# A two-layer attention trunk: gate sums and their biases issued earlier, `mem` loaded with `x`, GpSimd's distances held back

## The chip, the cores and the metric

The kernel runs on one core of one Trainium2 chip. The metric is the device time of one execution in microseconds (us), the median of three runs. The engines are TensorE (PE, matrix products), VectorE (DVE), ScalarE (ACT), GpSimd (POOL) and SyncE (SP, which here only issues transfers). Each engine runs its own instructions in order and waits on semaphores for the others.

## What is computed

A decoder trunk of two layers over 256 tokens of width 1024, all in float32:

```python
for i in range(DEPTH):                      # 0: forgetting attention (FoX), 1: block attention with ALiBi
    xn = rms_norm(h, norm_mix[i]); mn = rms_norm(mem, norm_mem[i])
    mk, mv = halves of mn @ w_mem_kv[i]     # 4 memory heads
    q, k, v, f_logit, qm = parts of xn @ w_in
    # FoX: log_f = log_sigmoid(f_logit + b_fgate); F = cumsum(log_f)
    #      logit[t, s] = q_t.k_s / 8 + F[t] - F[s], causal, softmax, times v      (12 heads)
    # MoBA with one block of 256: logit[t, s] = q_t.k_s / 8 - slope * (t - s), causal
    # memory: softmax(qm.mk / 8) @ mv
    h = h + concat(heads) @ w_out[i]
    gu = rms_norm(h, norm_ffn[i]) @ w_gate_up[i]
    h = h + (silu(gate) * up) @ w_down[i]
return rms_norm(h, norm_final)
```

## The kernel before

**Weights.** All weights lie in one stream in the order of their use, cut into units of 1 MB (128 partitions by 2048). `fetch` issues one unit from SP's queue into one of four buffers with the tag `raw`; the trace names them raw0, raw1 and so on. Products are made from split operands: `split` makes of each half unit a high part `hi` (a copy on ACT, L215) and a rest `lo` (a subtraction on DVE, L216). `weights` hands out a row of a unit and keeps five half units split ahead; `prod` turns each product into three: high by high, low by high, high by low. Units 5 and 6 are the first q and k group, 7 is `memT` (the transposed memory tokens, split into `x_mem`, L237 and L238), 8 and 9 the memory key and value weights, 10 is `mem` itself (only for its row norms), 11 the memory queries, 12 to 15 the second and third q and k groups.

**Order.** PE and SP run their instructions as the program writes them (`manual_schedule`). For DVE, ACT and POOL a scheduler at build time chose the order. Attention heads are generators (`attend`), kept in the list `active`; `step()` lets each of them go to its next `yield`, and is called after every second row of a q and k product. So score products, transposes and value products lie between the rows of the big products, and `IDLE` and `IDLE_MEM` say how many steps a pair of heads sits out.

**The first layer's mixer.** First the v products (they carry the 12 gate columns too), with the squared sums of `x` (`factor`: a Square on ACT with its sum, `me` on DVE, a power on POOL). From the gate columns come z, na, e, l and lf (log f). Then the first q and k group, `memory_heads` (the memory key and value products, the memory queries), and two more q and k groups. `gate_sums` is appended after the first q and k group: two products F (cumulative sums by row), a copy `fr`, a write of `fr` to DRAM (`fd`), three broadcast reads of it into `fk` (128 partitions by 12 heads by 256), and the products Fq with the copy `fq`. The write and the reads are on SP's queue, the reads behind the landing of the write. `bias` of a pair of heads then takes four DVE instructions (L510): fk minus fq plus mask, of 128 columns for the first query half into a buffer `bias`, of 256 for the second in place. In the second layer `bias` is two POOL instructions on `fk` (L505, distance times slope), which the scheduler has put in the first layer's attention, as soon as a pair's `fk` is free.

**Memory heads.** `mk` (L349) is the product of the memory keys and the spread factor `rsb_mem`; eight ACT copies and four subtractions (two on DVE, two on POOL) split it, four copies and four subtractions split the queries `xqm`, and the score product `s_m` of the first memory pair needs them. It stands in PE's program after the fourth row of the second q and k group.

```python
ENG = (nc.gpsimd, nc.vector)
def step():
    for g in list(active):
        if next(g, "end") == "end":
            active.remove(g)
```

Of the kernel before, what the change touches and what calls it, by code (L numbers as in the profile page):

```python
# [64 lines left out]
def _constants():  # L65


    i = np.arange(P)
    ident = np.eye(P, dtype=np.float32)
    prefix = np.concatenate(  # L70
        [np.where(i[:, None] <= i[None, :], -1.0, 0.0), np.full((P, P), -1.0)], axis=1
    ).astype(np.float32)
    dist = i[:, None] + P - np.arange(2 * P)[None, :]
    mask = np.where(dist < 0, NEG, 0.0).astype(np.float32)
    dist = np.where(dist < 0, 3e38, dist).astype(np.float32)
    return np.concatenate([ident, prefix, mask, dist], axis=1)


class Plan:


    def __init__(self, a):
# [5 lines left out]
        for i in range(2):  # L88
# [5 lines left out]
            for g in range(3):  # L94
                if g == MEM_AT[i]:
                    if i == 0:
                        U["memT", 0] = self.unit([memT], 0, KD, 0, S)
                        self.mkv(a, 0)
                        self.blocks.append(a["mem"][0].reshape(NT, P, D).transpose(1, 0, 2).reshape(-1))
                        self.shapes.append((NT, 1, D))  # L100
                        U["mem"] = len(self.shapes) - 1
# [37 lines left out]
def trunk(ctx: ExitStack, tc: tile.TileContext, plan, stream, x, gains, norm_final, b_fgate, square, out):  # L139
# [14 lines left out]
    prefix = sq[:, P:3 * P]  # L154
    mask = sq[:, 3 * P:5 * P]
    dist = sq[:, 5 * P:7 * P]
# [26 lines left out]
    raw_only = {U["xT"], U["memT", 0], U["memT", 1], U["mem"]}  # L183
# [66 lines left out]

    def inverse_root(ms, more, name):
# [4 lines left out]
        nc.gpsimd.tensor_tensor(rs, me, minus_half, op=ALU.pow)  # L256
# [49 lines left out]
    fk = cp.tile([P, H, S], F32, name="fk")  # L306
    mks = [cp.tile([P, 2, 2 * S], F32R, name=f"mk{p}") for p in range(HM // 2)]
# [15 lines left out]
    def mem_kv(i):  # L323
# [117 lines left out]
    def mixer(i, xs, rs):  # L441
# [14 lines left out]
        for k, t in order:  # L456
            v_tile(k, t)
            if i == 0 and (k, t) == (FACTORS_AT, 1):
                rs.extend(factor(h[t_], f"x0{t_}") for t_ in range(NT))
        if i == 0:  # L460
# [22 lines left out]
        def gate_sums():  # L483
            yield
            fb = bank("F_ps")
            fb.mm(fb.t[:H, 0:S], lf[:, 0], prefix)
            fb.mm(fb.t[:H, P:S], lf[:, 1], prefix[:, 0:P], stop=True)
            fr = ap.tile([P, 2, S], F32, tag="work", name="fr", bufs=WORK_BUFS)[:H, 0]
            nc.vector.tensor_copy(fr, fb.t[:H, :S])
            nc.sync.dma_start(fd, fr)  # L490
            for g in range(GATE_PARTS):
                hs = slice(g * (H // GATE_PARTS), (g + 1) * (H // GATE_PARTS))
                nc.sync.dma_start(fk[:, hs], fd[hs].unsqueeze(0).to_broadcast([P, H // GATE_PARTS, S]))
            gb = bank("Fq_ps")
# [291 lines left out]
```

## Time and profile before

| | |
|---|---|
| device time, median of 3 runs | 628.02 us (627.84 to 628.21) |
| profiled execution, its own time | 628.5 us |
| its span | 626.7 us |
| PE busy | 610.7 us, 97% of the span |
| DVE busy | 456.9 us, 73% |
| ACT busy | 393.1 us, 63% |
| POOL busy | 60.5 us, 10% |

The span is the profiled stretch from the first to the last instruction; the 1.8 us to its own time lie around it. PE is busy nearly throughout, so the idle time that is left on PE, and where, is what the rows below look at. The first layer's mixer runs from the start to about 130 us, its feed-forward layer to about 316 us, then follows the second layer.

### The profile page before, as it was taken

To read this page: it belongs to the slowest core of one execution; us is meant where nothing else is said; L and a number is where in the kernel's file an instruction comes from. 1 tells how busy PE (TensorE), PEld (TensorE's weight loads), DVE (VectorE), ACT (ScalarE), POOL (GpSimd) and SP (SyncE) were. 2 spreads that over 40 slices of the span, in tenths; PEclk is the share of its full clock that TensorE was granted. 3 is DMA by queue.
4 is the path that set the end of the run, shared out by engine and by line. 5 is a ranking of instruction groups with operands and counts; after the bars stand their busy time and mean duration, and the time that the engine had idled before them with its cause. 6 is when DMAs were issued, how large, how long until landed. Compare 5 with 4: busy or idle time off the path is not lost.

```text
span 626.7 us, 9569 instructions
## 1 busy us (share of the span) xinstructions
PE 610.7 (97%) x3636; PEld 532.8 (85%) x3636; DVE 456.9 (73%) x827; ACT 393.1 (63%) x734; POOL 60.5 (10%) x90
## 2 busy tenths in 40 slices
PE   7999899999999999999999999999999999999995
PEld 6999887788888888888899999877888888888884
DVE  5588999977667676668675689986866666666664
ACT  6789888575555555557467499865755555555542
POOL 2022354300000000000011032200000000000000
PEclk9999999999999999999999999999999999999998
DMA  8985731445555545555445642332455555555301
GB/s 291 369 313 196 311 135 69 157 140 216 170 191 201 195 171 177 197 202 187 166 186 202 246 146 80 135 134 101 158 182 198 202 188 173 185 193 202 136 0 67
DMA packets 17638, 112.31 MB, mean 179 GB/s; under 512 B 2220, under 2 KB 2744, under 8 KB 5432
## 3 DMA queue, kind: packets, MB, share of 16 engines
q1 hardware_dynamic: 17304, 111.42, 49.3%
q8 instruction: 28, 0.46, 0.3%
q10 hardware_dynamic: 288, 0.29, 0.1%
q14 instruction: 18, 0.15, 0.1%
HBM read 110.64 MB, written 1.06 MB: 178 GB/s over the span
## 4 chain that ended last, share of the span: by engine, by line
PE 83%; DVE 7%; ACT 5%; issue 2%; DMA 2%; POOL 0%; SPq 0%; POOLq 0%; ACTq 0%; DVEq 0%
PE gu L178 39%; PE d_acc L178 18%; PE qk_ps L178 8%; PE v_ps L178 5%; PE o_acc L178 5%; DMA raw<-in_stream 2%; DVE lo L216 2%; PE s_s L178 1%; ACT hi L215 1%; PE mv_ps L178 1%; PE qm_ps L178 1%; PE mk_ps L178 1%; ACT p_s L406 1%; ACT xq L362 1%; PE s_m L178 1%
## 5 line engine op out<-in xcount | busy, mean ns | idle before, releaser
L216 DVE TENSOR_TENSOR lo<-raw,hi 128x1024 fp32r<-128x1024 f32 (+3 forms) x201 | 240.6, 1205 | 74.0 <-ACT hi L215 68.9
L215 ACT ACTIVATE hi<-raw 128x1024 fp32r<-128x1024 f32 (+3 forms) x201 | 206.4, 1035 | 76.8 <-PE d_acc L178 47.8
L178 PE MATMUL gu<-x_ffn,hi 128*128 128x512 f32 x704 | 250.0, 398 | 0.4 <-DVE x_ffn L238 0.3
L178 PE MATMUL gu<-x_ffn,lo 128*128 128x256 f32 x704 | 198.3, 282 | 0.0
L178 PEld LDWEIGHTS gu<-x_ffn,hi 128*128 128x128 f32 x704 | 132.2, 188 | 33.3 <-DVE x_ffn L238 1.4
L178 PEld LDWEIGHTS gu<-x_ffn,lo 128*128 128x128 f32 x704 | 132.9, 189 | 1.0 <-ACT x_ffn L237 0.3
L178 PE MATMUL d_acc<-hi,h 128*128 128x512 f32 x348 | 107.7, 390 | 0.0
L178 PEld LDWEIGHTS d_acc<-hi,h 128*128 128x128 f32 x348 | 65.4, 188 | 13.7
L178 PE MATMUL qk_ps<-x_x,hi 128*128 128x256 f32 x384 | 72.3, 284 | 0.0
L178 PE MATMUL d_acc<-lo,h 128*128 128x512 f32 x174 | 68.0, 391 | 0.0
L178 PEld LDWEIGHTS qk_ps<-x_x,hi 128*128 128x128 f32 x384 | 60.9, 192 | 0.8 <-issue 0.8
L178 PE MATMUL qk_ps<-x_x,lo 128*128 128x256 f32 x192 | 54.4, 283 | 0.0
L641 ACT ACTIVATE gate<-gu 128x256 f32<-128x256 f32 x44 | 16.9, 384 | 58.9 <-PE gu L178 58.9
L641 ACT ACTIVATE up<-gu 128x256 f32<-128x256 f32 x44 | 16.9, 385 | 41.1 <-PE gu L178 40.9
L178 PE MATMUL o_acc<-hi,x_hT 128*128 128x512 f32 x128 | 41.8, 405 | 0.6 <-DVE x_hT L235 0.3
L178 PEld LDWEIGHTS d_acc<-lo,h 128*128 128x128 f32 x174 | 32.7, 188 | 7.0
L642 DVE TENSOR_TENSOR gate<-gu,gate 128x256 f32<-128x256 f32 x44 | 18.7, 424 | 27.1 <-ACT gate L641 27.1
L642 DVE TENSOR_TENSOR up<-gu,up 128x256 f32<-128x256 f32 x44 | 18.7, 425 | 26.1 <-ACT up L641 26.1
L178 PEld LDWEIGHTS qk_ps<-x_x,lo 128*128 128x128 f32 x192 | 36.8, 192 | 0.0
L178 PE MATMUL v_ps<-hi,x_x 128*128 128x384 f32 (+1 forms) x128 | 33.6, 344 | 0.6 <-ACT hi L215 0.6
L178 PEld LDWEIGHTS o_acc<-hi,x_hT 128*128 128x128 f32 x128 | 22.8, 188 | 6.4 <-issue 1.3
L406 ACT ACTIVATE p_s<-p_s,nmax_s 128x128 f32<-128x128 f32 (+1 forms) x48 | 21.4, 447 | 10.5 <-DVE nmax_s L396 10.3
(152 smaller groups left out, 751.5 us busy)
## 6 DMA issues: line engine op xcount, KB each, us to landing
raw<-in_stream SPq DMA_DIRECT2D x95, 1024.0 KB, 4.8
raw<-in_stream SPq DMA_DIRECT2D x4, 768.0 KB, 4.9
raw<-in_stream SPq DMA_DIRECT2D x2, 780.0 KB, 8.8
fk<-fd SPq DMA_DIRECT2D x3, 512.0 KB, 5.1
raw<-in_stream SPq DMA_DIRECT2D x3, 390.0 KB, 5.8
h<-in_x SPq DMA_DIRECT2D x2, 512.0 KB, 9.2
raw<-in_stream SPq DMA_DIRECT2D x1, 512.0 KB, 7.4
gfin<-in_norm_final SPq DMA_DIRECT2D x1, 512.0 KB, 3.4
```

Of the source, the lines that this page charges most:

```text
L178: nc.tensor.matmul(o, lhsT, rhs, start=self.fresh, stop=stop, skip_group_check=True)
L215: nc.scalar.activation(hi[:, c0:c1], src[:, c0:c1], AF.Copy)
L216: nc.vector.tensor_sub(lo[:, c0:c1], src[:, c0:c1], hi[:, c0:c1].bitcast(F32))
L362: nc.scalar.activation(dst[HOME[a], a], q[HOME[a]], AF.Copy)
L406: nc.scalar.activation(pr[:, a, c], src, AF.Exp, bias=nmax[:, a, j], scale=scale, accum_out=total[:, a, j])
L641: nc.scalar.activation(v[:, 1], b[s].t[:, S:], AF.Copy)
L642: nc.vector.tensor_add(v[:, 0], b[s].t[:, :S], v[:, 1])
```

## The change

It has four parts. The generator `gate_sums` is appended before the first q and k group, sits out two steps, and issues F, Fq and the write `fd` after the sixth of its eight rows; one step later it issues the three reads into `fk`; then each of six steps issues the four bias instructions of one pair, into a buffer of its own for the first half (`first_bias`). The write and the reads move from SP's queue to POOL's. The second half of the constant `prefix` (all -1) becomes a broadcast of one column. `mem` leaves the stream of units: it is loaded behind `x` into two buffers with the tag `probs`, its squared sums come right after those of `x`, and its factor is spread right after that of `x`. POOL's distances for the second layer may be issued only after the sixth power on POOL (`powers[5]`, the second factor of the first feed-forward layer). The tag of one small buffer changes (`"f"` to `"x"`).

```diff
     def load_x():
         for t in range(NT):
             nc.sync.dma_start(h[t], x[0, t * P:(t + 1) * P, :])
+        for t in range(NT):
+            nc.sync.dma_start(mem_t[t], mem[0, t * P:(t + 1) * P, :])
         nc.sync.dma_start(sq, square)
...
-        nc.gpsimd.tensor_tensor(rs, me, minus_half, op=ALU.pow)
+        powers.append(nc.gpsimd.tensor_tensor(rs, me, minus_half, op=ALU.pow))
...
-        if i == 0:
-            fetch_to(U["mem"] + 1)
-            rs_mem.extend(factor(raws[U["mem"]][:, t, 0], f"mem{t}") for t in range(NT))
-            rsb_mem.append(spread(rs_mem, "mem", (1.0,), "mem")[:, 0, :])
...
                 rs.extend(factor(h[t_], f"x0{t_}") for t_ in range(NT))
+                rs_mem.extend(factor(mem_t[t_], f"mem{t_}") for t_ in range(NT))
...
         def gate_sums():
+
+            yield
             yield
             fb = bank("F_ps")
-            fb.mm(fb.t[:H, 0:S], lf[:, 0], prefix)
-            fb.mm(fb.t[:H, P:S], lf[:, 1], prefix[:, 0:P], stop=True)
+            fb.mm(fb.t[:H, 0:P], lf[:, 0], prefix, stop=True)
+            fb.mm(fb.t[:H, P:S], lf[:, 0], minus_one.to_broadcast([P, P]))
+            fb.mm(fb.t[:H, P:S], lf[:, 1], prefix, stop=True)
             fr = ap.tile([P, 2, S], F32, tag="work", name="fr", bufs=WORK_BUFS)[:H, 0]
             nc.vector.tensor_copy(fr, fb.t[:H, :S])
-            nc.sync.dma_start(fd, fr)
-            for g in range(GATE_PARTS):
-                hs = slice(g * (H // GATE_PARTS), (g + 1) * (H // GATE_PARTS))
-                nc.sync.dma_start(fk[:, hs], fd[hs].unsqueeze(0).to_broadcast([P, H // GATE_PARTS, S]))
+            nc.gpsimd.dma_start(fd, fr)
...
             nc.scalar.activation(fq.rearrange("p t h -> p (t h)"), gb.t[:, :NT * H], AF.Copy)
+            yield
+            for g in range(GATE_PARTS):
+                hs = slice(g * (H // GATE_PARTS), (g + 1) * (H // GATE_PARTS))
+                nc.gpsimd.dma_start(fk[:, hs], fd[hs].unsqueeze(0).to_broadcast([P, H // GATE_PARTS, S]))
+            for h0 in range(0, H, 2):
+                yield
+                for j in range(h0, h0 + 2):
+                    for t, o in ((0, first_bias), (1, fk)):
+                        nc.vector.scalar_tensor_tensor(o[:, j], fk[:, j, :(t + 1) * P], fq[:, t, j:j + 1], mask[:, P - t * P:],
+                                                       op0=ALU.subtract, op1=ALU.add)
...
             b = fk[:, h0:h0 + 2]
-            if i == 1:
+            if i == 0:
+                return first_bias[:, h0:h0 + 2], b
+
+            with tc.issue_after(powers[NT * 3 - 1].ins):
                 for a in range(2):
                     nc.gpsimd.tensor_scalar(b[:, a], dist, -float(slopes[h0 + a]), NEG, op0=ALU.mult, op1=ALU.max)
-                return b[:, :, P:], b
...
             kb = [bank(f"qk_ps{i}{2 * g + a}") for a in range(2)]
+            if i == g == 0:
+                active.append(gate_sums())
...
                 rsb = spread(rs, f"x{i}", (DH ** -0.5, 1.0), "x")
                 if i == 0:
-                    active.append(gate_sums())
+                    rsb_mem.append(spread(rs_mem, "mem", (1.0,), "mem")[:, 0, :])
```

The orders that the scheduler chose change with it. On ACT, at the end of the v products (`v0`, `v1` are the scaled v, `e`, `l`, `na` the gate's small tiles, `hi6` the split of the second half of the first q and k group), before:

```order
L477 ACTIVATE v0_80<-v_ps000_144,rs_x00_295 128x384
L477 ACTIVATE v1_81<-v_ps010_146,rs_x01_302 128x384
L467 ACTIVATE e_329<-na_327 128x24
L469 ACT_TABLE_LOAD
L469 ACTIVATE l_331<-e_329 128x24
L215 ACTIVATE hi6_0_258<-raw6_166 128x1024
L215 ACTIVATE hi6_2_274<-raw6_166 128x1024
L237 ACTIVATE x_mem0_499<-raw7_188,gT_72 128x256 x8
```

and ACT at the same place in the change:

```order
L476 ACTIVATE v0_84<-v_ps000_151,rs_x00_302 128x384
L476 ACTIVATE v1_85<-v_ps010_153,rs_x01_309 128x384
L244 ACTIVATE junk_mem0_311,ms_mem0_312<-mem0_82 128x1024
L244 ACTIVATE junk_mem1_318,ms_mem1_319<-mem1_83 128x1024
L467 ACTIVATE na_348<-na_348 128x24
L468 ACT_TABLE_LOAD
L468 ACTIVATE na_348<-na_348 128x24
L216 ACTIVATE hi6_0_265<-raw6_173 128x1024
L216 ACTIVATE hi6_2_281<-raw6_173 128x1024
L238 ACTIVATE x_mem0_536<-raw7_195,gT_72 128x256 x7
L497 ACTIVATE fq_358<-Fq_ps_455 128x24
L238 ACTIVATE x_mem0_536<-raw7_195,gT_72 128x256
```

The two squared sums of `mem` now stand ahead of the gate's exponential and of the split `hi6`, and the copy `fq` stands inside the splits of the memory tokens. On DVE the two `me_mem` likewise stand ahead of the two `z`.

On DVE ahead of `mk0` (the product of memory keys and factor, which the first memory scores need), before:

```order
L216 TENSOR_TENSOR lo12_0_543<-raw12_371,hi12_0_542 128x1024
L216 TENSOR_TENSOR lo12_2_589<-raw12_371,hi12_2_588 128x1024
L254 TENSOR_SCALAR me_mem1_717<-ms_mem1_715 128x1
L216 TENSOR_TENSOR lo13_0_621<-raw13_429,hi13_0_620 128x1024
L216 TENSOR_TENSOR lo13_2_650<-raw13_429,hi13_2_649 128x1024
L216 TENSOR_TENSOR lo14_0_680<-raw14_431,hi14_0_679 128x1024
L216 TENSOR_TENSOR lo14_2_757<-raw14_431,hi14_2_756 128x1024
L349 TENSOR_TENSOR mk0_726<-mk_ps0_506,rsb_mem_724 128x512
```

and DVE there in the change:

```order
L217 TENSOR_TENSOR lo11_2_620<-raw11_327,hi11_2_619 128x1024
L506 SCALAR_TENSOR_TENSOR fk_87<-fk_87,fq_358,sq_74 128x256
L506 SCALAR_TENSOR_TENSOR first_bias_88<-fk_87,fq_358,sq_74 128x128 x2
L506 SCALAR_TENSOR_TENSOR fk_87<-fk_87,fq_358,sq_74 128x256 x2
L217 TENSOR_TENSOR lo12_0_656<-raw12_390,hi12_0_655 128x1024
L506 SCALAR_TENSOR_TENSOR first_bias_88<-fk_87,fq_358,sq_74 128x128 x2
L506 SCALAR_TENSOR_TENSOR fk_87<-fk_87,fq_358,sq_74 128x256 x2
L217 TENSOR_TENSOR lo12_2_689<-raw12_390,hi12_2_688 128x1024
L506 SCALAR_TENSOR_TENSOR first_bias_88<-fk_87,fq_358,sq_74 128x128 x2
L506 SCALAR_TENSOR_TENSOR fk_87<-fk_87,fq_358,sq_74 128x256 x2
L217 TENSOR_TENSOR lo13_0_723<-raw13_460,hi13_0_722 128x1024
L349 TENSOR_TENSOR mk0_750<-mk_ps0_543,rsb_mem_502 128x512
```

Between `lo8_0` (the first split of the memory weights) and `mk0` there now stand 20 of the 24 bias instructions, ten of each width, and eleven `lo`, two `qk`, four subtractions of q and k; before, no bias stood there, and twelve `lo`. (Units are numbered one lower from 11 on, since `mem` left the stream.)

On POOL, behind the last power of `mem`, in the change (`xq00`, `xk00` are subtractions for the first pair's q and k):

```order
L259 TENSOR_TENSOR rs_mem1_323<-me_mem1_321,minus_half_78 128x1
L492 DMA fd_86<-fr_452 12x256
L501 DMA fk_87<-fd_86 128x1024
L501 DMA fk_87<-fd_86 128x1024 x2
L364 TENSOR_TENSOR xq00_506<-qk00_504,xq00_506 64x256
L372 TENSOR_TENSOR xk00_507<-qk00_504,xk00_507 64x256
```

Before, POOL went from the powers of `x` straight to these subtractions; now the write and the three reads stand ahead of them, and the first read waits for the write. The twelve distances stand behind the powers of the first feed-forward layer.

## Rows read from the trace of the kernel before

**Rows 1.** Page, part 1: busy us, share of the span, instructions.

```profile
PE 610.7 (97%) x3636; PEld 532.8 (85%) x3636; DVE 456.9 (73%) x827; ACT 393.1 (63%) x734; POOL 60.5 (10%) x90
```

**Rows 2.** PE's waits from 25 to 130 us: total us, times, longest.

```profile
PE s_m L178 <- POOL xqm L364: 2.0, 1, 2.0
PE s_s L178 <- DVE pT_s L421: 0.8, 1, 0.8
PE o_m L178 <- ACT pT_m L420: 0.4, 1, 0.4
PE s_s L178 <- DVE nmax_s L396: 0.3, 1, 0.3
PE o_acc L178 <- DVE nmax_s L396: 0.2, 1, 0.2
```

**Rows 3.** Busy time by window: PE, PEld, DVE, ACT, POOL, PEclk, DMA share, GB/s.

```profile
26.00:28.00 2.00, 2.00 (x19) 2.00 (x18) 1.24 (x4) 1.58 (x3) 0.00 (x0) 1.00 0.99 418
...
80.00:100.00 20.00, 19.34 (x145) 16.07 (x144) 19.55 (x58) 15.59 (x43) 10.05 (x11) 1.00 0.30 107
```

**Rows 4.** Timeline of ACT: start, us, instruction, idle before it.

```profile
25.07 1.27 ACT L477 ACTIVATE v<-v_ps,rs_x 128x384 f32<-128x384 f32 x2 [0.17 <-POOL rs_x L256]
26.74 0.22 ACT L467 ACTIVATE e<-na 128x24 f32<-128x24 f32 x1 [0.41 <-DVE na L465]
...
28.41 1.99 ACT L215 ACTIVATE hi<-raw 128x1024 fp32r<-128x1024 f32 x2
30.55 3.31 ACT L237 ACTIVATE x_mem<-raw,gT 128x256 fp32r<-128x256 f32 x8 [0.15 <-DMA raw<-in_stream]
...
48.25 1.05 ACT L243 ACTIVATE junk_mem<-raw 128x1024 bf16<-128x1024 f32 x1
```

**Rows 5.** Timeline of PE.

```profile
30.76 0.38 PE L178 MATMUL qk_ps<-x_x,lo 128*128 128x256 f32 x1
...
42.77 0.82 PE L178 MATMUL F_ps<-sq,lf 128*12 128x256 f32 x4
43.52 0.84 PE L178 MATMUL Fq_ps<-lf,sq 128*128 128x12 f32 x6
...
64.22 1.18 PE L178 MATMUL s_m<-mk,xqm 128*128 128x256 f32 x8 [2.05 <-POOL xqm L364]
```

**Rows 6.** Timeline of DVE.

```profile
25.73 0.37 DVE L463 SCALAR_TENSOR_TENSOR z<-v_ps,rs_x,bfg 128x12 f32<-128x12 f32 x2 [0.64 <-POOL rs_x L256]
...
53.67 4.63 DVE L216 TENSOR_TENSOR lo<-raw,hi 128x1024 fp32r<-128x1024 f32 x4 [0.87 <-ACT hi L215]
58.22 0.69 DVE L349 TENSOR_TENSOR mk<-mk_ps,rsb_mem 128x512 f32<-128x512 f32 x1
...
107.63 0.61 DVE L510 SCALAR_TENSOR_TENSOR bias<-fk,fq,sq 128x128 f32<-128x128 f32 x2
108.16 0.87 DVE L510 SCALAR_TENSOR_TENSOR fk<-fk,fq,sq 128x256 f32<-128x256 f32 x2
```

**Rows 7.** Timeline of SP's queue, and landing of the reads into fk.

```profile
52.73 0.43 SPq L490 DMA_DIRECT2D fd<-fr  x1
58.54 1.30 SPq L493 DMA_DIRECT2D fk<-fd  x3
...
DMA to landing us min/median/max: 4.2/5.1/6.2
```

**Rows 8.** Timeline of DVE and of POOL where the two run at once or alone.

```profile
41.16 0.84 DVE L364 TENSOR_TENSOR xq<-qk,xq 64x256 fp32r<-64x256 f32 x1
62.45 0.42 DVE L372 TENSOR_TENSOR mk<-mk,mk 64x256 fp32r<-64x256 f32 x1 [0.81 <-ACT mk L369]
93.29 1.22 DVE L216 TENSOR_TENSOR lo<-raw,hi 128x1024 fp32r<-128x1024 f32 x1
...
40.12 1.60 POOL L364 TENSOR_TENSOR xq<-qk,xq 64x256 fp32r<-64x256 f32 x1 [14.40 <-ACT xq L362]
92.97 2.47 POOL L505 TENSOR_SCALAR fk<-sq 128x256 f32<-128x256 f32 x2 [2.17 <-issue]
```

More of the change, by code (lines that the diff above doesn't have):

```diff
@@ L69, in _constants @@
     ident = np.eye(P, dtype=np.float32)
-    prefix = np.concatenate(
-        [np.where(i[:, None] <= i[None, :], -1.0, 0.0), np.full((P, P), -1.0)], axis=1
-    ).astype(np.float32)
+    prefix = np.where(i[:, None] <= i[None, :], -1.0, 0.0).astype(np.float32)
     dist = i[:, None] + P - np.arange(2 * P)[None, :]
@@ L138, in trunk @@
 @with_exitstack
-def trunk(ctx: ExitStack, tc: tile.TileContext, plan, stream, x, gains, norm_final, b_fgate, square, out):
+def trunk(ctx: ExitStack, tc: tile.TileContext, plan, stream, x, mem, gains, norm_final, b_fgate, square, out):
     nc = tc.nc
@@ L153, in trunk @@
     ident = sq[:, 0:P]
-    prefix = sq[:, P:3 * P]
-    mask = sq[:, 3 * P:5 * P]
-    dist = sq[:, 5 * P:7 * P]
+    prefix = sq[:, P:2 * P]
+    mask = sq[:, 2 * P:4 * P]
+    dist = sq[:, 4 * P:6 * P]
     slopes = _slopes()
@@ L160, in trunk @@
     nc.gpsimd.memset(minus_half, -0.5)
+    minus_one = cp.tile([P, 1], F32, name="minus_one")
+    nc.gpsimd.memset(minus_one, -1.0)
+    mem_t = [ap.tile([P, 2, 512], F32, tag="probs", name=f"mem{t}", bufs=3).rearrange("p a s -> p (a s)") for t in range(NT)]
     def load_x():
@@ L182, in trunk @@
     U = plan.U
-    raw_only = {U["xT"], U["memT", 0], U["memT", 1], U["mem"]}
+    raw_only = {U["xT"], U["memT", 0], U["memT", 1]}
     halves = [(i, j * (sh[0] // 2), sh[0] // 2) for i, sh in enumerate(plan.shapes) if i not in raw_only for j in range(2)]
@@ L306, in trunk @@
     fk = cp.tile([P, H, S], F32, name="fk")
+    first_bias = cp.tile([P, H, P], F32, name="first_bias")
     mks = [cp.tile([P, 2, 2 * S], F32R, name=f"mk{p}") for p in range(HM // 2)]
@@ L496, in gate_sums @@
                 for u in range(t + 1):
-                    gb.mm(gb.t[:, t * H:(t + 1) * H], prefix[:, (t - u) * P:(t - u + 1) * P], lf[:, u], stop=u == t)
+                    gb.mm(gb.t[:, t * H:(t + 1) * H], prefix if u == t else minus_one.to_broadcast([P, P]), lf[:, u], stop=u == t)
             nc.scalar.activation(fq.rearrange("p t h -> p (t h)"), gb.t[:, :NT * H], AF.Copy)
+            yield
[8 more added lines that the diff above has]
+                                                       op0=ALU.subtract, op1=ALU.add)
         def bias(h0):
             b = fk[:, h0:h0 + 2]
-            if i == 1:
+            if i == 0:
+                return first_bias[:, h0:h0 + 2], b
+            with tc.issue_after(powers[NT * 3 - 1].ins):
                 for a in range(2):
                     nc.gpsimd.tensor_scalar(b[:, a], dist, -float(slopes[h0 + a]), NEG, op0=ALU.mult, op1=ALU.max)
-                return b[:, :, P:], b
-            b0 = ap.tile([P, 2, P], F32, tag="bias", name=f"bias{h0}", bufs=1)
-            for a in range(2):
-                for t, o in ((0, b0), (1, b)):
-                    nc.vector.scalar_tensor_tensor(o[:, a], b[:, a, :(t + 1) * P], fq[:, t, h0 + a:h0 + a + 1], mask[:, P - t * P:],
-                                                   op0=ALU.subtract, op1=ALU.add)
-            return b0, b
+            return b[:, :, P:], b
         hT = xposed(f"hT{i}")
@@ L634, in gu @@
             if first:
-                rsb.append(spread(rs, f"f{i}", (1.0,), "f")[:, 0])
+                rsb.append(spread(rs, f"f{i}", (1.0,), "x")[:, 0])
             if kk == 0:
@@ L774 @@
     arrays = {
-        "stream": np.concatenate(plan.blocks), "x": a["x"], "gains": gains,
+        "stream": np.concatenate(plan.blocks), "x": a["x"], "mem": a["mem"], "gains": gains,
         "norm_final": a["norm_final"], "b_fgate": a["b_fgate"], "square": square,
```

12 lines of the change are left out of this document (4 added, 8 removed).

## The prediction

> **What bounds the kernel now.** I read the page first: PE is busy for 610.7 of 626.7 us [rows 1], so nothing but PE's idle time can be won. The list of PE's waits between 25 and 130 us says where it is in the first mixer: 2.05 us before the first memory scores `s_m`, and later 0.8, 0.4, 0.3 and 0.2 us, behind DVE or ACT [rows 2]. The windows show why the later ones are there: from 80 to 100 us DVE is busy for 19.55 of 20 us, so the attention heads go at DVE's pace [rows 3]. All that an earlier gate chain can win here is 2.05 + 1.7 = 3.75 us.
>
> The second thing to see is how tight the queues are ahead of that. In the first q and k group PE uses the low half of unit 6 at 30.76 [rows 5]. ACT began that unit's split at 28.41 [rows 4], and a split half takes about 1.0 us on ACT (1.99 for two) and 1.14 on DVE (four in the 4.55 us from 53.67 to 58.22) [rows 4, 6]. So PE takes it the moment it is there, and whatever delays ACT here delays PE.
>
> **What the change costs, step by step.**
>
> *Squares of `mem` ahead of the gate.* ACT ends its two v copies at 26.34 [rows 4]. Now two squares of 1.05 follow, to 28.44. DVE's two `me_mem` stand ahead of `z`, so `z` waits for them, and with it, queued behind on DVE, the scaled v and `na`, for which ACT's exponential waits. From `z` (25.73) to the exponential (26.74) took 1.01 us, from there to the split of unit 6 1.67 us [rows 4, 6]. So the split starts at 28.44 + 0.05 + 1.01 + 1.67 = 31.2 instead of 28.41, and PE gets the low half at 33.5: **2.7 us of new idle time**, in a place where there was none. Could the load of `mem` make it worse? It is 1 MB in front of units 6 and 7, less 64 KB of the smaller constants: 0.98 MB at 418 GB/s [rows 3] is 2.4 us. Unit 7 landed at 30.55, since ACT waited for it [rows 4]; unit 6, a megabyte ahead, at about 28.0. With 2.4 us more it lands at 30.4, before ACT comes to it: hidden, by 0.8 us. Squares and factor no longer stand among the memory products; there ACT and DVE win about 2 us, but see what is late next.
>
> *F and Fq* cost PE 1.45 us (42.77 to 43.52, and from there as long again less 0.1) [rows 5] and only change place. The product with the broadcast column has as many columns as the half of `prefix` that it replaces: nothing, plus at most 0.1 us for one more instruction. The new spread of `mem`'s factor is the old one, earlier.
>
> *ACT and DVE up to the memory weights.* ACT ends unit 6 at 33.2, seven splits of `x_mem` (3.31 us for eight [rows 4]) at 36.1, and then `fq` makes it wait for PE: 23 products of 0.12 us after 33.5, F and Fq, 37.7. The last `x_mem` and the first half of unit 8 bring it to 39.1, and DVE starts `lo8_0` at 39.2.
>
> *The biases ahead of `mk`.* This is the dear part. From `lo8_0` to `mk` DVE now has eleven splits of 1.14 (12.5 us), ten biases of 128 columns at 0.265 (107.63 to 108.16 for two) and ten of 256 at 0.40 (0.87 for two, less the overlap of the next) [rows 6], 6.6 us, two `qk` of 0.6, 1.2 us, and four subtractions of 0.42 [rows 8], 1.7 us. Two of the four ran at 0.84 when POOL subtracted beside them [rows 8]; POOL's own four come a little later now and meet splits and biases instead, so I leave the 0.85 us in. Sum 22.9 us of work; my count of the moments when ACT has not yet delivered gives 1.6 us of waiting. So `mk` starts at 39.2 + 22.9 + 1.6 = 63.7, against 58.22 [rows 6].
>
> *From `mk` to `s_m`.* Behind `mk` DVE still has `qm` 0.6, two splits 2.3, two subtractions 0.85, four biases 1.3 and the subtraction for `xqm` 0.4, with `mk` itself 6.1 us; with 0.3 of waiting 6.4 us, against 6.0 before (58.22 to 64.22 [rows 5, 6]). ACT's copies for it run beside. So `s_m` starts at 70.1. The same sum made for the kernel before gives 64.6 where the trace has 64.22, so I take 0.4 off: **69.7, that is 5.5 us later.** PE itself would be there at 64.9 (64.22 less its wait of 2.05, and the 2.7 lost above), so its wait grows from 2.05 to about 4.8 us. Queued behind the waiting `s_m` in PE's program is everything else of the layer.
>
> *After that* DVE has less to do than before, by some 7 us of biases and plus two splits that were put off, so the waits of 0.8, 0.4, 0.3 and 0.2 us should go: **1.7 us back**, or nothing if the put-off splits fill the room.
>
> *POOL and SP.* The reads into `fk` wait on POOL for the write, and behind them stand POOL's first subtractions, needed only by the first self scores after `s_m`: free. `fr` is there at 37.5. Before, 5.8 us went by from the issue of the write to that of the reads, and the reads took 4.2 to 6.2 us to land [rows 7]. What POOL takes to issue a transfer no row shows; the bounds are these rows and 3 us more (the 1.30 us of SP's three issues, doubled). By the rows the first part of `fk` lands at 47.5, the last at 49.5 to 50.8; DVE comes to the first bias at 48.7, so I take no wait. Units 10 to 14 come earlier, since SP no longer waits on `fd` and no buffer is held by `mem`; the work that needs them is late anyway.
>
> *The distances* leave the mixer, where POOL is no bottleneck, and put 12 × 1.2 us [rows 8] on POOL beside the feed-forward layer, where PE sets the pace. A DVE split that ran under two distances took 1.22 us, no longer than others [rows 8]. I take zero; with every distance blocking DVE it would be 14 us of DVE time, spread over a layer in which the splits are five half units ahead.
>
> On this the Trainium skill has a rule (SBUF — State Buffer, "SBUF: two separate sides"): DVE and GpSimd share a port pair as an exclusive lock, taken by a DVE instruction with two SBUF inputs against a GpSimd instruction that reads SBUF, and the later one waits for the whole other. The split beside two distances disagrees, the subtraction of 0.84 beside POOL's 1.60 fits [rows 8].
>
> **The sum.** +5.5 − 1.7 = +3.8 us. The profiled execution took 628.5 us and would take 632.3; it lies 0.5 above the median of 628.02, so the forecast is **631.8 us**, 0.6% slower.
>
> **Rivals.**
>
> 1. *The mixer gets its cover (not slower).* If `mk` starts by 58.5, `s_m` is ready when PE is (64.9), both kinds of wait go, and only the 2.7 us remain: 628.0 − 3.75 + 2.7 = 626.9. For it speaks that ACT no longer waits for a load and for `rsb_mem` ahead of `mk`. Against it: DVE enters at 39.2 and has 22.9 us of work before `mk`, 3.6 us too much without any waiting. It needs the scheduler's bias instructions to run much shorter than their rows. The break-even is `mk` at 60.0. If the delay of 2.7 did not show either, it would be 624.3.
> 2. *The delay at unit 6 is overlapped.* If `z` did not sit behind `me_mem`, or ACT made up for it, everything starts 2 to 2.7 us earlier: 629.1 to 629.8, or no difference with the later waits gone as well.
> 3. *`fk` lands late.* With POOL's issues at 3 us more, the first bias waits 1 to 4 us, DVE holds `mk` back by the same, and the time is 633 to 636.
> 4. *POOL's subtractions block DVE.* Four that each hold DVE for 0.8 us (half of the 1.60 that one took beside DVE [rows 8]) in place of the 0.85 counted: +2.3, 634.1. The rule named above speaks for it.
> 5. *Nothing comes back later.* DVE stays the bound to 122 us with the splits put off: 628.0 + 5.5 = 633.5.
>
> **Chances.** The forecast with its own range of 630 to 633, 0.47; rival 1 0.17, rival 2 0.14, rival 3 0.08, rival 4 0.05, rival 5 0.09. The bound for a difference that a measurement of this kernel can tell is 0.2%, 1.3 us. Faster: the better part of rival 1, 0.11. Within 0.2% (626.8 to 629.3): the rest of rival 1 and half of rival 2, 0.13. Slower: 0.76. The range takes in rival 1 at 626.9 and most of rival 3: 626.9 to 635.0.
>
> **What would show it.** In the first q and k group PE waits 2.5 to 3 us for `lo` of unit 6, its split on ACT starting near 31. `mk` starts near 63 on DVE, with no gap on DVE ahead of it longer than 0.6 us, and `s_m` near 69.7 after a wait of over 4 us. From there to the feed-forward layer PE's waits sum to under 0.7 us. The feed-forward layers and the second layer have the length that they had. A gap on DVE ahead of the first `first_bias` would mean rival 3; `mk` before 60 would prove me wrong.

## The result, and the profile after

The changed kernel took 634.94 us (median of 4 runs, 633.64 to 636.61), the kernel before 628.12 us on the same chip (4 runs, 627.84 to 629.48): ratio 1.0084, 95% interval 1.0062 to 1.0107. That is 6.8 us slower, where 3.8 were forecast. The profiled execution took 634.49 us with a span of 632.7. On the chips of the experiments the kernel before ran from 627.8 to 632.2 us (its runs with a mean granted clock of 0.996 or more at 627.8 to 630.0, the others at 629.1 to 632.2), so each experiment is compared by its ratio to runs of the same chip, and traces are read for waits and not for spans. The changed kernel was not run on those chips, and the median of the kernel before lies 1.7 to 2.3 us higher there (629.83 to 630.38) than here, so the ratio of an experiment and the 1.0084 can differ by 0.3% through what they are divided by alone.

Of the changed kernel, the page's part 1, as in [rows 1]:

```profile
PE 612.7 (97%) x3638; PEld 535.4 (85%) x3638; DVE 458.3 (72%) x827; ACT 392.8 (62%) x734; POOL 65.9 (10%) x95
```

and PE's waits from 25 to 140 us (total, times, longest), as in [rows 2]:

```profile
PE s_m L179 <- POOL xqm L364: 4.8, 1, 4.8
PE s_m L179 <- DVE xqm L364: 1.7, 1, 1.7
PE qk_ps L179 <- DVE lo L217: 0.9, 1, 0.9
PE qk_ps L179 <- ACT hi L216: 0.4, 1, 0.4
PE o_acc L179 <- DVE x_hT L236: 0.2, 1, 0.2
```

PE is busy for 2 us more, and idle for 4 more. Of the waits of [rows 2] the later ones are down to 0.2, but the first has become 4.8 us and a second of 1.7; two new ones stand in the first q and k group. The timeline of ACT (start, us, instruction, idle before it), for [rows 4]:

```profile
25.17 1.05 ACT L244 ACTIVATE junk_mem<-mem 128x1024 bf16<-128x1024 f32 x1
...
28.50 0.22 ACT L467 ACTIVATE na<-na 128x24 f32<-128x24 f32 x1 [1.16 <-DVE na L466]
...
30.16 1.99 ACT L216 ACTIVATE hi<-raw 128x1024 fp32r<-128x1024 f32 x2
```

and that of PE, for [rows 5]:

```profile
31.26 0.38 PE L179 MATMUL qk_ps<-x_x,hi 128*128 128x256 f32 x1 [0.36 <-ACT hi L216]
32.52 0.39 PE L179 MATMUL qk_ps<-x_x,lo 128*128 128x256 f32 x1 [0.88 <-DVE lo L217]
...
68.79 1.19 PE L179 MATMUL s_m<-mk,xqm 128*128 128x256 f32 x4 [4.85 <-POOL xqm L364]
71.64 1.19 PE L179 MATMUL s_m<-mk,xqm 128*128 128x256 f32 x4 [1.66 <-DVE xqm L364]
76.84 1.12 PE L179 MATMUL s_s<-xk,xq 128*128 128x256 f32 x8
...
135.88 0.36 PE L179 MATMUL gu<-x_ffn,lo 128*128 128x256 f32 x1
```

Before, all eight products of `s_m` ran in one piece from 64.22 [rows 5]; now four run, and PE waits again for the other four. The timeline of DVE, for [rows 6]:

```profile
27.38 0.15 DVE L257 TENSOR_SCALAR me_mem<-ms_mem 128x1 f32<-128x1 f32 x1 [0.89 <-ACT junk_mem L244]
27.48 0.37 DVE L464 SCALAR_TENSOR_TENSOR z<-v_ps,rs_x,bfg 128x12 f32<-128x12 f32 x2
...
49.39 0.61 DVE L506 SCALAR_TENSOR_TENSOR first_bias<-fk,fq,sq 128x128 f32<-128x128 f32 x2 [0.82 <-DMA fk<-fd]
...
63.33 0.69 DVE L349 TENSOR_TENSOR mk<-mk_ps,rsb_mem 128x512 f32<-128x512 f32 x1
...
65.78 0.84 DVE L372 TENSOR_TENSOR mk<-mk,mk 64x256 fp32r<-64x256 f32 x1
66.63 0.98 DVE L506 SCALAR_TENSOR_TENSOR first_bias<-fk,fq,sq 128x128 f32<-128x128 f32 x2
...
68.04 0.99 DVE L372 TENSOR_TENSOR mk<-mk,mk 64x256 fp32r<-64x256 f32 x1
69.06 0.85 DVE L506 SCALAR_TENSOR_TENSOR fk<-fk,fq,sq 128x256 f32<-128x256 f32 x1
69.83 1.21 DVE L217 TENSOR_TENSOR lo<-raw,hi 128x1024 fp32r<-128x1024 f32 x1
71.07 0.76 DVE L364 TENSOR_TENSOR xqm<-qm,xqm 64x256 fp32r<-64x256 f32 x2
```

and that of POOL, for [rows 7, 8]:

```profile
41.24 1.64 POOL L501 DMA_DIRECT2D fk<-fd  x3 [3.44 <-DMA fd<-fr]
...
64.55 2.65 POOL L372 TENSOR_TENSOR mk<-mk,mk 64x256 fp32r<-64x256 f32 x2 [15.38 <-ACT mk L369]
68.02 0.72 POOL L364 TENSOR_TENSOR xqm<-qm,xqm 64x256 fp32r<-64x256 f32 x1 [0.83 <-ACT xqm L362]
68.90 0.73 POOL L364 TENSOR_TENSOR xqm<-qm,xqm 64x256 fp32r<-64x256 f32 x1 [0.16 <-ACT xqm L362]
```

`mk` is late by 5.1 us, behind twenty biases. Between `mk` and DVE's share of `xqm` stand four more, `qm`, two splits and two subtractions, several of them longer than alone while POOL subtracts. And windows of 2 us with their granted clock (seventh column), for [rows 3], with the window in which POOL makes the distances:

```profile
66.00:68.00 2.00, 0.00 (x0) 0.00 (x0) 1.99 (x4) 1.89 (x6) 1.19 (x2) 1.00 0.55 131
68.00:70.00 2.00, 1.19 (x4) 0.89 (x4) 1.94 (x4) 1.93 (x4) 1.44 (x2) 0.72 0.93 393
70.00:72.00 2.00, 0.36 (x2) 0.39 (x3) 1.97 (x4) 1.62 (x2) 0.00 (x0) 0.50 0.00 0
72.00:74.00 2.00, 2.00 (x11) 2.00 (x11) 1.60 (x5) 1.36 (x5) 0.00 (x0) 0.50 0.00 0
74.00:76.00 2.00, 2.00 (x12) 2.00 (x12) 2.00 (x4) 0.68 (x4) 0.00 (x0) 0.58 0.28 33
76.00:78.00 2.00, 2.00 (x19) 2.00 (x18) 1.16 (x7) 0.90 (x1) 0.00 (x0) 1.00 0.62 246
...
140.00:160.00 20.00, 19.92 (x108) 17.05 (x108) 17.60 (x25) 14.01 (x24) 17.44 (x13) 1.00 0.55 204
```

After the long wait PE is granted 0.50, 1.2 instead of 2.4 GHz, until 75 us: 11 products in 2 us where 19 fit at 1.00. The distances cost PE nothing: it is busy for 19.92 of 20 us.

**Where the 6 us of the two profiled executions are.** From `s_m` to the first `s_s` 3.89 us went by before (64.22 to 68.11 on PE's timeline), now 8.05; from there to the first product of the feed-forward layer 61.74 (to 129.85), now 59.04; from that to the end 496.8, as before. So: `s_m` starts 4.57 later (1.77 because PE comes later, 2.80 of longer waiting); the second half comes 2.85 us behind the first, where it followed after 0.48 (four products at 0.12) before: 2.37; the products from there to `s_s` take 5.20 instead of 3.41, at the lower clock: 1.79; and 2.70 come back later. 4.57 + 2.37 + 1.79 − 2.70 = 6.03.

### The profile page after: what moved, and what is told of

Its sections match the earlier page's. It is cut to its first block, busy times and chain, and to the rows that moved or that the text cites. A ratio compares the mean times of both kernels' runs of the same rounds, so it can differ in the third digit from the quotient of the medians.

```text
span 632.7 us, 9573 instructions
## 1 busy us (share of the span) xinstructions
PE 612.7 (97%) x3638; PEld 535.4 (85%) x3638; DVE 458.3 (72%) x827; ACT 392.8 (62%) x734; POOL 65.9 (10%) x95
## 4 chain that ended last, share of the span: by engine, by line
PE 81%; DVE 7%; ACT 6%; DMA 3%; issue 2%; SPq 0%; POOLq 0%; POOL 0%; ACTq 0%; DVEq 0%
PE gu L179 38%; PE d_acc L179 18%; PE qk_ps L179 7%; PE v_ps L179 5%; PE o_acc L179 5%; DVE lo L217 3%; PE s_s L179 1%; DMA fk<-fd 1%; ACT hi L216 1%; PE qm_ps L179 1%; PE mv_ps L179 1%; PE mk_ps L179 1%; ACT p_s L406 1%; ACT x_ffn L238 1%; DMA raw<-in_stream 1%
## 5 line engine op out<-in xcount | busy, mean ns | idle before, releaser
L217 DVE TENSOR_TENSOR lo<-raw,hi 128x1024 fp32r<-128x1024 f32 (+3 forms) x201 | 241.0, 1205 | 69.7 <-ACT hi L216 64.7
L179 PE MATMUL qk_ps<-x_x,hi 128*128 128x256 f32 x384 | 74.0, 288 | 0.4 <-ACT hi L216 0.4
L179 PEld LDWEIGHTS qk_ps<-x_x,hi 128*128 128x128 f32 x384 | 62.2, 195 | 1.3 <-issue 0.8
L650 DVE TENSOR_TENSOR up<-gu,up 128x256 f32<-128x256 f32 x44 | 18.7, 424 | 25.7 <-ACT up L649 25.6
L318 POOL MEMSET xk<- 64x256 f32 x24 | 7.4, 309 | 195.7 <-PE d_acc L179 162.8
```

Source lines behind the costliest of these rows:

```text
L179: nc.tensor.matmul(o, lhsT, rhs, start=self.fresh, stop=stop, skip_group_check=True)
L217: nc.vector.tensor_sub(lo[:, c0:c1], src[:, c0:c1], hi[:, c0:c1].bitcast(F32))
L318: nc.gpsimd.memset(dst[HOME[1 - a], a, S:].bitcast(F32), 0.0)
L650: nc.vector.tensor_add(v[:, 0], b[s].t[:, :S], v[:, 1])
```

## The experiments

Theory A: the biases ahead of `mk` hold the memory scores. Rival B: the reads of `fk` on GpSimd's queue land late. Rival C: the early load and squares of `mem` carry the loss. Rival D: the distances do. The intervals are of 95%.

**e1_bias_late: the biases back at the pair's call**

```diff
         def gate_sums():
...
-            for h0 in range(0, H, 2):
-                yield
-                for j in range(h0, h0 + 2):
-                    for t, o in ((0, first_bias), (1, fk)):
-                        nc.vector.scalar_tensor_tensor(o[:, j], ...
         def bias(h0):
             if i == 0:
+                for j in range(h0, h0 + 2):
+                    for t, o in ((0, first_bias), (1, fk)):
+                        nc.vector.scalar_tensor_tensor(o[:, j], ...
                 return first_bias[:, h0:h0 + 2], b
```

> The changed kernel, with one part undone: each pair's four biases are issued again when the pair's scores are (still from first_bias and fk, still from the sums of the early gate chain, still with the parts of fk on GpSimd's queue), so most of them stand behind mk on DVE. Theory A (the biases ahead of mk hold the memory scores): PE waits 2 to 2.5 us before the first s_m instead of 4.85, and 0 to 0.5 before the second half instead of 1.66; the granted clock stays at 1.00 between 65 and 80 us; the 2.7 us given back later (no biases left behind mk) are lost again. Sum 634.9 - 4.3 - 1.8 + 2.7 = 631.5, and as low as 630. Rival B (fk lands late through GpSimd's queue, and whoever needs it waits): the time stays at 634 to 635. Rival C (the squares of mem and the start of the first q/k group carry the loss): 633.5 to 635.

Ratio 1.0018 (1.0005 to 1.0032): most of the loss is gone, four fifths of it if the 1.0084 holds for this chip too. On this chip itself e3, which keeps the biases early, took 635.78 us and e1 631.10. PE's timeline:

```profile
67.29 1.21 PE L179 MATMUL s_m<-mk,xqm 128*128 128x256 f32 x8 [1.14 <-POOL xqm L364]
```

All eight products run in one piece again, after 1.14 us. Rival D can't be right, since the distances are those of the change, and neither can rival B as the carrier of the loss: queue and reads are the same. Late reads could still hold up the biases where these are early; the trace of the change has 0.82 us for that. What this trace shows of the rest stands in the first q and k group, where PE waited 1.2 us for `hi` and 0.9 for `lo`, and then ran at 0.65 and 0.50:

```profile
34.00:36.00 2.00, 2.00 (x14) 2.00 (x14) 2.00 (x6) 1.68 (x5) 0.00 (x0) 0.65 0.60 152
36.00:38.00 2.00, 2.00 (x11) 1.57 (x11) 0.70 (x2) 0.00 (x0) 0.00 (x0) 0.50 0.90 369
```

**e2_gate_only: the kernel before with the gate chain and the early biases alone**

```diff
+            if i == g == 0:
+                active.append(gate_sums())    # gate_sums, bias and first_bias of the change
...
             if g == 0:
                 rsb = spread(...)
-                if i == 0:
-                    active.append(gate_sums())
```

> The kernel before, with the gate chain and the biases of the change alone: sums in the first q/k group, fd and fk on GpSimd's queue, all 24 biases ahead of mk as DVE comes to them; mem stays in the stream with its squares late, the distances stay in layer 2's attention. Theory A (the biases ahead of mk): z near 25.7 and no wait in the first q/k group, mk at 61.5 to 63.5, 4 to 7 us of PE idle ahead of s_m, perhaps the lower clock behind it, ratio to before 1.004 to 1.008. Rival C (mem's early load and squares carry the loss): mk under 60, ratio 0.998 to 1.002. Rival D (the distances in layer 1's feed-forward carry it): the same ratio as C.

Ratio 1.0083 (1.0063 to 1.0102), the whole loss, with `mem` and the distances left where they were: rivals C and D fall. The wait is at another place than I expected: `me_mem` now stands behind the biases on DVE, so the spread of `mem`'s factor on PE waits. So e2 shows that early biases are enough for a loss of this size, but by another wait than in the change; that the two ratios are equal does not make it one path. DVE's timeline and PE's wait:

```profile
60.92 0.21 DVE L254 TENSOR_SCALAR me_mem<-ms_mem 128x1 f32<-128x1 f32 x2
```

```profile
PE rsb_ps_mem L178 <- POOL rs_mem L256: 7.0, 1, 7.0
```

**e7_early_part: the change with its first stretch put right** (constants loaded ahead of `mem`, squares and spread of `mem` where they were)

```diff
         for t in range(NT):
             nc.sync.dma_start(h[t], x[0, t * P:(t + 1) * P, :])
-        for t in range(NT):
-            nc.sync.dma_start(mem_t[t], mem[0, t * P:(t + 1) * P, :])
         nc.sync.dma_start(sq, square)
         nc.sync.dma_start(bfg, ...)
+        for t in range(NT):
+            nc.sync.dma_start(mem_t[t], mem[0, t * P:(t + 1) * P, :])
...
+        if i == 0:
+            rs_mem.extend(factor(mem_t[t_], f"mem{t_}") for t_ in range(NT))
+            rsb_mem.append(spread(rs_mem, "mem", (1.0,), "mem")[:, 0, :])
         mk = ap.tile(...)
```

> The changed kernel, with its first stretch put right twice: sq and b_fgate stand ahead of mem on SP's queue, and the squares of mem and their spreading stand where they stood before (behind the products of mk); the biases stay ahead of mk. Theory A: z at 25.5 to 26 (27.48 now), no wait in the first q/k group; the 20 biases still push mk to 62 to 63.5, so that the wait ahead of s_m grows by what the first stretch gives back; ratio to before 1.005 to 1.0075. Rival C (the first stretch carries the loss): wait ahead of s_m under 3 us, ratio 0.999 to 1.002.

Ratio 1.0085 (1.0065 to 1.0104). `z` ran at 25.41, as expected, but PE still waited 0.8 and 0.9 us in the first group. ACT's timeline says for what:

```profile
30.56 2.00 ACT L216 ACTIVATE hi<-raw 128x1024 fp32r<-128x1024 f32 x2 [2.38 <-DMA raw<-in_stream]
```

The unit itself isn't there before 30.56, since the megabyte of `mem` is loaded ahead of it (in e2, without that, ACT had it at 27.60). And further on the spread waited 7.1 us as in e2; `mk` started at 67.07. So where the biases are early, the squares of `mem` have to be early too.

**e4_squares_late: only the squares of `mem` held back on ACT**

```diff
+                if i == g == 0 and k == 3:
+                    with tc.issue_after(his[11].ins):    # the second hi of the unit behind the gate
+                        rs_mem.extend(factor(mem_t[t_], f"mem{t_}") for t_ in range(NT))
```

> The changed kernel, with the two squares of mem held back on ACT until the second split of the unit behind the gate's exponential (hi_0, hi_2) has been issued, so that ACT's order is v, exponential, Ln, hi_0, hi_2, squares. Theory A: PE's 1.24 us of waiting in the first q/k group (0.36 for hi and 0.88 for lo) go; the gate chain and so the parts of fk come about 1 us earlier, and the memory scores with them by 0 to 1 us: 633.7 to 634.9, with the wait ahead of s_m at 4.8 to 6 us. Rival C (the squares of mem carry most of the loss, since all behind them on ACT and DVE comes later): the wait ahead of s_m falls to 2 or 3 us and the time to 630 to 631.

Ratio 1.0069 (1.0048 to 1.0091). It doesn't answer its question: with the squares moved, the scheduler put one rest of the memory tokens (`x_mem`) behind eight biases on DVE, at 56.27, and PE waited 4.9 us for it among the memory products. But DVE's timeline shows a second hold of the late `z`:

```profile
28.18 0.37 DVE L464 SCALAR_TENSOR_TENSOR z<-v_ps,rs_x,bfg 128x12 f32<-128x12 f32 x2 [3.09 <-DMA bfg<-in_b_fgate]
```

`z` needs the gate's bias, whose small load stands behind the megabyte of `mem` on SP's queue. In the changed kernel it was issued at 16.44 and landed 9.7 us later, at 26.1, 1.3 us before `z` ran at 27.48; in e4 it was issued at 17.5 and landed 10.6 us later, so `z` came 0.7 later than in the change. In the kernel before it had been issued at 14.6 and had landed 11.0 us later, at 25.6.

**e8_bfg_first: only the load order of e7**

> The changed kernel with sq and b_fgate loaded ahead of mem, and nothing else in the code; in ACT's order this puts the squares of mem behind the gate's Ln instead of ahead of its exponential, still ahead of hi_0 of the next unit. It tells the two reasons of the late z apart, of which each can hide the other: behind me_mem on DVE (27.48 in the changed kernel), or behind the landing of b_fgate (28.18 where the squares were held back). If both must go, z is at 25.5 to 26 here, and the gate chain 1.7 us earlier, while hi_0 still waits for the squares and PE for hi_0 and lo: 1 to 2.5 us. Ratio to before 1.006 to 1.009, since the biases stay ahead of mk.

Ratio 1.0073 (1.0052 to 1.0094). `z` started at 24.82; the scheduler itself now put the squares behind the gate's Ln. PE waited 0.2 and 0.9 in the first group, and 4.4 and 1.6 ahead of the halves of `s_m`: the biases are still there.

**e10_late_bfg: the edits of e1 and e8 together**

> The changed kernel with each pair's biases issued with the pair's scores again (as in the run that measured 1.0018) and sq and b_fgate ahead of mem. What was left of the loss there stood in the first q/k group (1.2 us for hi, 0.9 for lo, and 3 us at a granted clock of 0.50 behind them). Theory A: z at 25 instead of 28.2, hi_0 still behind the squares of mem; the two waits fall to 1 us or less and the clock stays at 1.00; ratio to before 0.998 to 1.001. Rival (the first stretch was chance, not the order of the loads): 1.001 to 1.003 again.

Ratio 0.9995 (0.9982 to 1.0009): against the median of the kernel before the loss is gone; the lowest run is still 1.0 us above its lowest (629.16 for 628.14). The waits in the first group came to 0.7 and 0.9, more than the 1 us expected (the split there follows straight behind the squares of `mem`, which end at 30.4 in its trace), but the clock stayed at 1.00:

```profile
34.00:36.00 2.00, 2.00 (x18) 1.85 (x18) 2.00 (x6) 1.90 (x5) 0.00 (x0) 1.00 1.00 389
36.00:38.00 2.00, 2.00 (x18) 1.74 (x17) 1.14 (x3) 0.55 (x3) 0.59 (x1) 1.00 0.97 369
```

That the order of the loads makes the difference to e1 is not shown: the two intervals overlap, and the traces of the change, of e3 and of e5, whose loads stand as in e1, have only 1.24 and 1.25 us of waiting in this group and no lower clock behind it.

**e3_keep_busy: products without use in the waits ahead of `s_m`**

```diff
         for a in range(2):
+            if name == "m00":
+                for _ in range((5, 1)[a]):
+                    sb[a].fresh = True
+                    sb[a].mm(sb[a].t, ident, sq[:, :512], stop=True)
+                sb[a].fresh = True
```

> The changed kernel, with six products added that are not in the reference: 5 of ident by sq (128x512) into the bank of the first memory scores ahead of its four products, and 1 ahead of the second half; the scores then begin afresh in the same bank. They need nothing that is late, so they run while PE would otherwise wait for xqm, and they end before it is there if one takes no more than 0.9 us. Theory A, with a fall of the clock that follows from the idle time: PE's granted clock stays at 1.00 (now 0.50 from 69 to 75 us), the q/k products behind the memory scores stand 0.12 us apart instead of 0.21, and the time falls by 1.7 to 1.8 to about 633.2. Rival (the fall of the clock costs nothing, because PE waits for something else there, or it falls for another reason than the idle time): 634.5 to 635.

Ratio 1.0094 (1.0070 to 1.0118), no better than the change. The clock did what was expected, the time didn't. Windows:

```profile
70.00:72.00 2.00, 1.46 (x6) 0.63 (x6) 1.97 (x3) 1.39 (x2) 0.70 (x1) 1.00 0.46 193
...
74.00:76.00 2.00, 2.00 (x19) 2.00 (x18) 2.00 (x5) 0.00 (x0) 0.00 (x0) 1.00 0.30 61
```

PE's waits from 60 to 140 us:

```profile
PE s_m L179 <- DVE xqm L364: 1.2, 1, 1.2
PE o_m L179 <- ACT pT_m L425: 0.7, 1, 0.7
PE qk_ps L179 <- ACT p_m L411: 0.4, 1, 0.4
PE qk_ps L179 <- DVE qk L574: 0.3, 1, 0.3
```

From the second half of `s_m` (72.62) to `s_s` (76.1) it took 3.5 us instead of 5.2, and from there to the feed-forward layer (136.9) 60.8 instead of 59.0: 64.24 us from the one to the other in both traces. What PE won at the full clock it gave back in waits for ACT and DVE, which the low clock had covered. So the 1.79 us in the account above are no loss by themselves: the heads go at DVE's pace. (That all of it lies 1.0 us later than in the change is not the filling's work: already the first q and k group was 1.5 us later in this trace, 32.73 for 31.26.)

**e5_scores_late, e11_late_bfg_scores, e12_before_scores: the memory scores one step later in PE's order**, in the change, in e10, and in the kernel before

```diff
-IDLE_MEM = (1, 1)
+IDLE_MEM = (2, 1)
```

> The changed kernel, with one number changed: the memory scores stand one step (two k of the second q/k group, some 5.8 us of PE) later in PE's order; the biases stay where they are. Theory A, if the delay of mk is a matter of one late operand: the 6.5 us ahead of the two halves of s_m fall to under 1, the granted clock stays at 1.00, and the time to 626.5 to 628.5 (634.9 - 6.5 - 1.8, and up to 1.5 of new waits behind). Theory A', if DVE is behind as a whole and not mk alone: PE waits as long at the next operand (nmax and p of the memory heads, the q/k of the next pair), 631 to 634. Rival B (fk lands late): the pair's scores, which need the bias, wait instead, 632 to 635.

> The kernel of the run with late biases and b_fgate ahead of mem, and the memory scores one step later in PE's order as well. Theory A (one late operand, mk, behind it DVE with room): the 1 to 2 us ahead of s_m go, ratio 0.996 to 0.999. Rival A' (DVE is full from 40 to 120 us, and PE waits for it at whatever comes next): 0.999 to 1.002, with the waits moved to s_s, pT and o.

> The kernel before, with the memory scores one step later in PE's order and nothing of the change. It shows what that step is worth without the change: the 2.05 us that PE waits for xqm go if the wait is of one late operand, ratio 0.997 to 0.998; if DVE is full behind it and the wait comes back at s_s and pT, ratio 0.999 to 1.003.

e5: 1.0044 (1.0028 to 1.0060), half of the loss gone, between the two theories. The waits from 60 to 110 us:

```profile
PE s_m L179 <- DVE xqm L364: 2.1, 1, 2.1
PE pT_m L417 <- DVE p_m L410: 1.3, 2, 1.0
PE s_s L179 <- ACT pT_s L420: 0.8, 1, 0.8
PE s_m L179 <- POOL xqm L364: 0.6, 1, 0.6
```

A step of PE's work covers part of the late operand; DVE's backlog is met at the next. e11: 1.0064 (1.0046 to 1.0082): with no wait left at `s_m`, PE waited 3.0 us at `pT_m` for `p_m` and the clock fell to 0.91 in the mean from 80 to 100 us. That is worse than rival A' had it. e12: 0.9987 (0.9976 to 0.9998): the fastest version of all, but by less than the 0.2% that can be told from no change; its wait at `s_m` was gone, and 3.6 us stood at `pT_m` and `pT_s` instead.

**e9_after_xqm: all 24 biases issued after the last `xqm`**, on top of e7's edits

```diff
+            while len(xqm_at) < HM // 2:
+                yield
             for h0 in range(0, H, 2):
-                yield
+                with tc.issue_after(xqm_at[-1].ins):
...
```

> The changed kernel with both losses taken out and everything else kept: sq and b_fgate ahead of mem, squares of mem where they stood before, and all 24 biases issued on DVE only after the last xqm of the memory heads (early gate sums, early fk, mem loaded with x, distances in the feed-forward layer stay). Theory A: no wait in the first q/k group, mk at 57.5 to 59, 1.5 to 2.5 us ahead of s_m, granted clock 1.00 throughout, and since the sums and fk are there in time the later waits no larger than before: ratio to before 0.997 to 1.001. Rival B (fk on GpSimd's queue costs by itself): the pair's first nmax waits for a DMA, ratio 1.003 or more. Rival D (distances in the feed-forward layer cost by themselves): the stretch from the first gu to the end longer than before's 496.9 us by 2 or more.

Ratio 1.0125 (1.0106 to 1.0143): the slowest of all, where I expected no change. Windows:

```profile
60.00:80.00 20.00, 16.13 (x119) 15.45 (x118) 13.74 (x40) 13.24 (x30) 4.17 (x8) 0.91 0.37 139
```

PE's waits from 60 to 140 us:

```profile
PE s_m L179 <- POOL xqm L368: 2.8, 1, 2.8
PE s_s L179 <- ACT pT_s L425: 2.4, 1, 2.4
PE qk_ps L179 <- ACT p_m L411: 1.7, 1, 1.7
PE pT_m L422 <- DVE nmax_s L401: 1.1, 1, 1.1
```

DVE is busy for 13.74 of 20 us from 60 to 80, where the change has 18.61 and the kernel before 18.79. Between `mk` and `xqm` DVE now stands idle for 3.0 us in gaps, where e1 has 0.2 because biases and splits fill them, and the biases then stand among the softmax of the heads. The loss lies there: against e1 the first `s_s` is only 0.7 us late (71.92 for 71.21), and from it to the feed-forward layer 68.2 us went by for 62.0. A part of theory A falls with it: it isn't enough that the biases are out of `mk`'s way. That the empty gaps are the reason is argued from these rows, and no run took it apart; e9 also has the squares of `mem` late, which e1 has not.

**e13_before_again: the kernel before, profiled on another chip**

> The kernel before, unchanged, profiled on another chip. On the chips of the experiments its runs lie at 628.1 to 628.7 where the mean granted clock was 0.996 to 0.998, and at 629.0 to 632.2 where it was 0.992 to 0.995; the profile that the prediction was made from is one of the first kind. A profile of the second kind would show where the clock falls. Theory A: in the mixer, behind a stall of PE that is there in both kinds (the 2 us ahead of s_m, or one in the first q/k group when the loads come later), for some 3 us at 0.50, in a place where experiments with late biases keep 1.00. Rival: at the program's ends, where no experiment changes anything, so that the difference between the kinds has nothing to do with the change. Ratio 0.998 to 1.002 in either case.

Ratio 1.0003 (0.9985 to 1.0021). The profiled execution was one at clock 0.997, so it doesn't show where the others lose theirs; that stays open. It shows how well a trace repeats: `s_m` at 64.0 and the feed-forward layer at 129.6, 0.2 us from the trace of the prediction. The first stretch repeats less well: the v copies began at 23.54, for 25.07 in [rows 4]. Against it e10's profile still has 1.6 us of waiting in the first group, and its layer starts at 131.8: e10 equals the kernel before in the median, not in its best runs.

## Why the prediction was right, and where its size was off

The direction came from the mechanism that the runs show, biases ahead of `mk`. The size did not: 634.94 lies above the forecast's own range of 630 to 633, and inside the wider one, which was drawn around the rivals, 626.9 to 635.0, by 0.06 us; two of the four runs lie above 635.0. That is luck.

- *The squares and unit 6*: the mechanism was there (`z` straight behind `me_mem`), the size wasn't: 1.24 us of new idle time for 2.7, the split at 30.16 for 31.2. The v copies began at 23.61, 1.5 us earlier than in [rows 4], because the weights ahead of them had landed earlier (ACT's last wait for one was 2.08 us for 3.29). That much differs without any edit: the kernel before, profiled again, has 23.54 (e13), and with the loads of the change the copies began between 23.39 (e5) and 25.08 (e3), and PE waited up to 2.08 us in this group (e1). And there were three holds of similar length where I saw one: the squares, the gate's bias queued behind `mem` (e4, e8), which no step of mine looked at, and the unit itself. Of that I had said that it lands at 30.4 and is hidden by 0.8 us behind the squares: it had landed by 30.16 in the change, by 29.72 in e8 and at 30.56 in e7, where with the squares gone ACT waited 2.38 us for it.
- *The biases ahead of `mk`*: `mk` at 63.33 for 63.7, with 0.82 us of DVE waiting for `fk`. Right, and shown by e1 to be the main cause: 1.0084 falls to 1.0018 without them. With the gate chain alone they give 1.0083 (e2), by the other wait named there.
- *From `mk` to `s_m`* is the term that was mis-sized. For the first half it is right: a wait of 4.85 for about 4.8, the start at 68.79 for 69.7 (PE too was there 0.9 earlier than forecast). But the step took all eight products as one, ready when DVE's own subtraction for `xqm` is done, 6.4 us after `mk` starts. The first four go with POOL's share and came earlier; the other four need DVE's, which was done about 8.1 us after `mk` (71.07 + 0.4 − 63.33). They started at 71.64, where 69.7 + 0.48 = 70.18 was implied: 1.46 us more. No term had the lower clock either.
- *POOL's subtractions* (rival 4) are what made that stretch long. Between `mk` and `xqm` the four rows of 0.84, 0.98, 0.99 and 0.85 exceed what they take alone (0.42, 0.61, 0.42, 0.48) by 1.7 us together, beside POOL's 2.65 and two of 0.7. On the rule weighed in the prediction (Trainium skill, SBUF — State Buffer, "SBUF: two separate sides"), by which the later instruction is held until the other ends, the trace agrees in part. POOL's two for `mk` took 1.78 and 0.90, so when the four rows began, 0.55, 0.57, 0.70 and 0.57 us of POOL's were left, and they took 0.42, 0.37, 0.57 and 0.37 longer. But the splits beside the distances, which ran without a gap, took 1.21 to 1.23 and only once 1.42, where 1.23 is their time with POOL idle.
- *What comes back later*: 2.70 for 1.7, again with luck. With the clock held at 1.00 only 0.94 came back (61.74 to 60.80 in e3); the other 1.76 is the slack that PE's low clock gave DVE, and it pays for the 1.79 lost to that clock.
- *POOL's queue*: no wait was counted, 0.82 us came. `fk` landed after 8.1 to 12.1 us, where [rows 7] had 4.2 to 6.2. The same 1.5 MB now ran among the weights, and from another queue; no run tells the two apart. Rival 3 was that far right.
- *F and Fq, the distances*: nothing, as said; from the feed-forward layer to the end 496.8 us for 496.9.

The profiled execution missed its forecast of 632.3 by 2.2 us. By these traces 1.46 of them are the late second half of `s_m`; most of the rest is the 1.7 that was to come back, of which 0.94 did. The lower clock and the slack that it gave DVE cancel (e3, one trace).

## What to carry to other kernels

Work that is "ready early" is not free to be issued early: on an engine that runs in order it goes ahead of an operand for which PE waits, so sum that queue up to the *last* instruction that PE's group needs, with the lengths that its rows have beside GpSimd's work. But don't push such work behind everything either: where the engine is near its limit the best place is the gaps, and both extremes lost here (with the gate's bias loaded ahead of `mem` in all three: 1.0073 with the biases ahead of `mk`, 1.0125 with them behind `xqm` and the squares late too, 0.9995 at the pair's call). And when a large load moves forward on a queue, look at the small ones right behind it.

## What the runs showed of the hardware that was not expected

- PE was granted 0.50 (1.2 GHz) for some 6 us after a wait of 4.85 us, and for some 3 us after two waits of 1.21 and 0.87 us that lay 0.4 us apart (e1); two of 0.68 and 0.88 at the same place (e10), and one of 2.05 in the kernel before, left it at 1.00. Behind one of 2.80 (e9) it was 0.61 and 0.53.
- The fall behind the 4.85 us cost nothing that could be won back: from the second half of `s_m` to the feed-forward layer both traces have 64.24 us, with it and without it (e3).
- The gate's bias, 12 numbers to each of 128 partitions, landed 9.7 us after its issue when it stood behind 1 MB, and 10.4 us after it when it stood ahead (e8): what the order moved was its issue, from 16.44 to 14.27. (In the kernel before: 11.0, from 14.6.)
